# Moving the loads of x, half of the low parts, one norm and one sigmoid in a transformer block with 32 experts

## The chip, the cores and the metric

One Trainium2 chip, one core. The metric is the device time of one execution in microseconds (us). The kernel works in float32 throughout; its projections run as pairs of rounded operands (fp32r), as told below.

## What is computed

The reference is one encoder block over 256 tokens of width 1024: a joint projection, differential attention (4 heads) and neighbourhood attention (8 heads) on its columns, a gated merge, a residual with layer norm, and then a mixture of 32 experts with the best 4 for each token.

```python
proj = x @ w_in + b_in                          # 1024 -> 5120 columns
q_da, k_da, v_da, q_na, k_na, v_na, gate_pre = split(proj)
q_da, k_da = rope(q_da), rope(k_da)
a  = diff_attention(q_da, k_da, v_da, lam, lam_init, subln_g)   # softmax, RMS norm per head
nb = neighbourhood_attention(q_na, k_na, v_na, rpb)             # softmax with a position bias
g  = sigmoid(gate_pre)                          # two gates of width 1024
merged = g[0] * (a @ w_branch_da) + g[1] * (nb @ w_branch_na)
x = layer_norm(alpha * x + merged @ w_out)
x = layer_norm(alpha * x + moe(x))              # top 4 of 32, clamped SwiGLU
```

## The kernel before

The weights come in through a ring of SBUF tiles of 2 MB each, loaded by SP's queue in the order of their use. The first 28 pieces of 1 MB are called blocks here: blocks 0 to 19 are the ten column groups of `w_in` (two blocks a group: the first and the second half of the 1024 input rows), 20 to 23 the two branch matrices, 24 to 27 `w_out`. Behind them come the experts' weights, 403 MB. `refill` loads a ring tile again once TensorE is through with both of its blocks.

For accuracy each block is split into a rounded high part and the remainder, the low part: `split(i)` works in two halves of 128x1024, `act` on ScalarE (ACT) makes the high part, `tt` on VectorE (DVE) subtracts it from the block to make the low part. There are two tiles of split parts (`SPL = 2`), so block i's split can start when TensorE has done block i - 2. x goes the same way (`XH`, `XL`). A projection is then three products: high by high, low by high, high by low. Of a block's 48 matmuls (24 wider ones where the result is a value matrix, groups 2 and 5, that is blocks 4, 5, 10 and 11) the first half needs the first half of the split alone.

At the start, `feed` issues block 0 in four pieces of 256 KB, and after each the matching quarter of x (`load_x`); blocks 1 and 2 come in two pieces each. Block 0 uses the first half of x, block 1 the second.

Between the blocks the loop at the end of this stage calls what `at(key, ...)` has put down: after block 2 and block 4 the rotary embedding (`rope`: 14 DVE products and sums, seven for each pair of heads), after 6 to 9 the scores and the softmax of a differential head and after 7 to 10 its transpose, after 12 the RMS norm of the heads in two pairs (`da_norm`: a matmul of ones with the squares, a square root on ACT, a reciprocal, a scaling and a split on DVE), after 12, 13, 15 and 16 the neighbourhood heads (`na_bias` adds a mask to the bias on GpSimd, `na_softmax` goes to DVE and ACT), after 18 the sigmoid of gate "a", after 20 the router's loads. A planner of the framework orders the instructions of each engine's queue from their place in the program and from its own estimate of when they are ready; the order isn't written out by hand up to the end of `w_out`. On each engine instructions then run strictly in queue order. The order of the expert stage is written out by hand.

GpSimd (POOL in the profile) has little to do: the constants, two small loads into `gbx` at the start, and the eight bias adds of `na_bias`. `tp` and `pv` are PSUM tiles with one buffer each, `tp` used by the transposes, `pv` by the attention outputs.

The profile gives all of `act` as line L43 and all of `tt` as L46; the names of the tiles tell them apart: `sp` are the split parts, `qb`, `tm`, `qq` the rotary embedding, `pr`, `w`, `sm` the softmax, `tm<-tm` at L389 the reciprocal of the norm.

Of the kernel before, what the change touches and what calls it, by code (L numbers as in the profile page):

```python
# [9 lines left out]
F32 = mybir.dt.float32  # L10
# [3 lines left out]
ALU = mybir.AluOpType  # L14
# [17 lines left out]
def block_kernel(ctx: ExitStack, tc: tile.TileContext, x, xT, w_in, cols_in, b_v, lam_v,  # L32
# [9 lines left out]
    def act(o, i, f=AF.Copy, **kw):  # L42
        return nc.scalar.activation(o, i, f, **kw)  # L43

    def tt(o, a, b, op):
        return nc.vector.tensor_tensor(out=o, in0=a, in1=b, op=op)  # L46
# [41 lines left out]
    def feed(where=ring_tile):  # L88

        if not queue:  # L90
            return
        u = queue.pop(0)
        t = where()
        home[u] = where
        for s in range(2):
            ring[2 * u + s] = t[:, s * 2048:(s + 1) * 2048]
        if 2 * u < N1:
            for i in (2 * u, 2 * u + 1):
                src, k = chunks[i]
                v = ring[i].rearrange("p (k c) -> p k c", k=k)  # L100
                if i == 0:
                    for j in range(4):
                        nc.sync.dma_start(v[:, j], src[:, j])
                        load_x(j)
                elif i < 3:
                    for j in range(2):
                        nc.sync.dma_start(v[:, 2 * j:2 * j + 2], src[:, 2 * j:2 * j + 2])
                else:
                    nc.sync.dma_start(v, src)
            return  # L110
        kind, e, c = expert_unit(u)
        if kind == "m1":
            nc.sync.dma_start(t.rearrange("p (r c) -> p r c", r=2), m1c(e, c // 2))
        else:
            v, src = t.rearrange("p (k c) -> p k c", k=4), m2c(e, c // 2)
            n = 2 if e == NE - 1 else 4
            for k in range(0, 4, n):
                nc.sync.dma_start(v[:, k:k + n], src[:, k:k + n])
# [37 lines left out]
        t = splp.tile([128, 2, 2, 1024], F32R, name="sp", tag="sp")  # L156
        return [[t[:, u, n] for n in range(2)] for u in range(2)]

    def split(i):

        if i < N1 and (i, 0) not in parts:
            t = split_tile()
            for u in range(2):
                s = ring[i][:, u * 1024:(u + 1) * 1024]
                ws = t[u]
                act(ws[0], s)
                tt(ws[1], s, ws[0].bitcast(F32), ALU.subtract)
                k = chunks[i][1] // 2
                parts[i, u] = [w.rearrange("p (k c) -> p k c", k=k) for w in ws]

# [52 lines left out]
    def load_x(q):  # L223
        nc.sync.dma_start(xTt[:, 2 * q:2 * q + 2],
                          xT[256 * q:256 * q + 256, :].rearrange("(k p) t -> p k t", p=128))
# [15 lines left out]

    XH = big.tile([128, 8, T], F32R, name="XH", tag="xh")
    XL = big.tile([128, 8, T], F32R, name="XL", tag="xl")
    w0 = [[w.rearrange("p (k c) -> p k c", k=2) for w in ws] for ws in split_tile()]
    for j in range(4):
        u, r = divmod(j, 2)
        v = ring[0][:, j * 512:(j + 1) * 512]
        parts[0, u] = w0[u]
        act(w0[u][0][:, r], v)
        tt(w0[u][1][:, r], v, w0[u][0][:, r].bitcast(F32), ALU.subtract)  # L250
        s = slice(2 * j, 2 * j + 2)
        act(XH[:, s], xTt[:, s])
        tt(XL[:, s], xTt[:, s], XH[:, s].bitcast(F32), ALU.subtract)


    nlam = p1.tile([128, 1], F32, name="nlam")
# [125 lines left out]

    def da_norm(u):
        hh = slice(2 * u, 2 * u + 2)
        ms = pp.tile([128, 2, T], F32, name="tp", bufs=1)
        nc.tensor.matmul(ms, lhsT=ones, rhs=sq[:, hh], start=True, stop=True)
        rs = p1.tile([128, 2, T], F32, name="tm", tag="w", bufs=2)
        act(rs, ms, AF.Sqrt, scale=1.0 / 128.0, bias=eps)
        nc.vector.reciprocal(out=rs, in_=rs)  # L389
        nc.vector.scalar_tensor_tensor(out=rs, in0=aT[:, hh], scalar=gcol, in1=rs,  # L390
                                       op0=ALU.mult, op1=ALU.mult)
        act(AH[:, hh], rs)
        tt(AL[:, hh], rs, AH[:, hh].bitcast(F32), ALU.subtract)
# [20 lines left out]
    def na_softmax(h):  # L414
# [4 lines left out]
        sm = p1.tile([128, 4, 2], F32, name="sm", bufs=4)  # L419
        nc.vector.tensor_reduce(out=sm[:, 0], in_=s, axis=AX.X, op=ALU.max)  # L420
        nc.vector.tensor_scalar(sm[:, 1], sm[:, 0], -1.0, None, op0=ALU.mult)
        w = p1.tile([128, 2, T], F32, name="w", bufs=2)
        W["n", h] = w
        for q in range(2):
# [94 lines left out]
    def router_loads():  # L519
        nc.sync.dma_start(wr, w_router.rearrange("(k p) e -> p k e", p=128))  # L520
        nc.sync.dma_start(br[:, 0], b_router.rearrange("(o e) -> o e", o=1))

        for j, src in enumerate((ln1_g, ln1_b)):
            nc.gpsimd.dma_start(gbx[:, j].rearrange("p (c r) -> p c r", r=2), src.rearrange("(c p r) -> p c r", p=128, r=2))

    def router_fold():

# [15 lines left out]
    at(8, evac_t, 3, qk_na[:, 0:4])  # L543
    at(10, evac_t, 4, qk_na[:, 4:8])
    at(12, evac_v, 5, 1)
    at(12, da_norm, 0)
    at(12, da_norm, 1)
    at(12, na_alloc)
    for p, i in enumerate((12, 13, 15, 16)):
# [8 lines left out]
    at(14, gate, "a", 6, 0, AF.Identity)  # L558
    at(16, gate, "a", 7, 1, AF.Identity)
    at(17, gate_alloc, "b")  # L560
    at(18, lambda: act(G["a"], G["a"], AF.Sigmoid))
    at(18, gate, "b", 8, 0, AF.Sigmoid)
    at(20, gate, "b", 9, 1, AF.Sigmoid)
    at(21, gate_a, 0)
# [6 lines left out]
    at(23, lambda: preload(AF.Sqrt, G["b"][0:1, 7, 0:1]))  # L571

    for i in range(N1):
        if i + 1 < N1:
            split(i + 1)
        if i < 20:
            (proj_v if i // 2 in (2, 5) else proj_t)(i)
# [594 lines left out]
```

## Time and profile before

| | |
|---|---|
| time, median of 3 runs | 1151.42 us (1150.56 to 1152.11) |
| the profiled execution, its time | 1151.79 us |
| its span, first to last instruction | 1149.7 us |
| TensorE busy in the span | 93% |
| DVE, ACT, GpSimd busy | 32%, 22%, 2% |
| mean granted TensorE clock | 0.992 |
| read from memory | 437.86 MB, 382 GB/s over the span |

TensorE's busy share is that of pipelined matmuls whose ends are modelled, so 93% doesn't say that TensorE is at its peak. The projections, the attention and `w_out` end at about 202 us; the experts take the rest. In the rows below a line of the timeline gives the start, the duration, the engine, the line of the kernel, the operation, the output and its inputs, the shape and the count of instructions merged into it; in square brackets stands how long the engine had been idle before it and what ended that.

### The profile page before, as it was taken

How to read it: one execution, taken by the hardware profiler on the slowest of the kernel's cores; microseconds unless marked ns; L12 is line 12 of the kernel's file. 1: busy time of each engine (PE TensorE's matmuls, PEld its weight loads, DVE VectorE, ACT ScalarE, POOL GpSimd, SP SyncE). 2: the span in 40 equal slices, each digit the busy share in tenths (PEclk: the TensorE clock that was granted, in tenths of full speed). 3: DMA queues.
4: the chain of work that ended last, by engine and by line, in shares of the span. 5: the costliest groups of instructions: out<-in, count | busy, mean ns of one | idle time of the engine just before them, and what ended most of it. 6: DMA issues, size and time to landing. Idle time of an engine off the chain costs nothing.

```text
span 1149.7 us, 13448 instructions
## 1 busy us (share of the span) xinstructions
PE 1071.6 (93%) x5596; PEld 518.7 (45%) x5596; DVE 370.6 (32%) x786; ACT 258.3 (22%) x519; POOL 21.3 (2%) x30
## 2 busy tenths in 40 slices
PE   8999999999999999999999999998998899999884
PEld 8888898543334333333333333333333333333221
DVE  6977757223222222222222222222221222222213
ACT  5475853311111112122111111111111111111011
POOL 0001100000000000000000000000000000000001
PEclk9999999899999999999999999999999999999998
DMA  9953468799999999999999999999999999999991
GB/s 336 385 178 105 171 229 350 287 428 422 427 427 425 430 410 427 426 428 427 425 430 427 428 426 426 427 428 428 428 427 428 425 429 428 428 426 426 429 408 57
DMA packets 50787, 439.83 MB, mean 383 GB/s; under 512 B 5666, under 2 KB 8866, under 8 KB 23458
## 3 DMA queue, kind: packets, MB, share of 16 engines
q1 hardware_dynamic: 50098, 437.86, 91.9%
q8 instruction: 46, 0.75, 0.3%
q0 software_dynamic: 336, 0.54, 0.2%
q10 hardware_dynamic: 288, 0.52, 0.1%
q14 instruction: 19, 0.16, 0.0%
HBM read 437.86 MB, written 1.05 MB: 382 GB/s over the span
## 4 chain that ended last, share of the span: by engine, by line
DMA 45%; PE 44%; issue 4%; DVE 3%; ACT 2%; SPq 0%; POOL 0%; POOLq 0%; ACTq 0%
DMA ring<-in_w_dram 43%; PE sc L805 17%; PE tp L850 8%; PE pj L285 5%; PE pj L469 2%; PE tp L740 2%; PE sc L824 1%; PE pv L740 1%; DMA ring<-in_w_in_dram 1%; PE pj L873 1%; PE pj L300 1%; PE sc L510 1%; DVE tm L46 1%; ACT sp L43 1%; PE pv L884 1%
## 5 line engine op out<-in xcount | busy, mean ns | idle before, releaser
L805 PE MATMUL sc<-ring,XS 128*64 128x512 f32 x2048 | 473.7, 600 | 34.9 <-DMA ring<-in_w_dram 31.1
L805 PEld LDWEIGHTS sc<-ring,XS 128*64 128x64 f32 x2048 | 137.8, 137 | 305.0 <-issue 250.0
L850 PE MATMUL tp<-ring,hsas 128*64 128x512 f32 x1024 | 234.6, 598 | 12.2 <-DMA ring<-in_w_dram 11.7
L850 PEld LDWEIGHTS tp<-ring,hsas 128*64 128x64 f32 x1024 | 69.1, 136 | 150.7 <-issue 121.0
L813 DVE COPY hsas<-sc 128x512 f32<-128x512 f32 x32 | 22.1, 692 | 306.8 <-PE sc L805 306.8
L43 ACT ACTIVATE XS<-tp,gbx 128x128 f32<-128x128 f32 x64 | 25.8, 453 | 361.6 <-PE tp L740 359.8
L285 PE MATMUL pj<-XH,sp 128*128 128x256 f32 x512 | 96.3, 287 | 4.6 <-DVE sp L46 4.1
L285 PEld LDWEIGHTS pj<-XH,sp 128*128 128x128 f32 x512 | 80.1, 191 | 9.3 <-DVE sp L46 5.3
L46 DVE TENSOR_TENSOR sp<-ring,sp 128x1024 fp32r<-128x1024 f32 (+1 forms) x58 | 68.2, 1189 | 27.5 <-ACT sp L43 27.2
L771 DVE TENSOR_SCALAR GT<-pv,slotp 128x256 fp32r<-128x256 f32 x32 | 15.5, 484 | 186.7 <-PE pv L769 186.7
L43 ACT ACTIVATE sp<-ring 128x1024 fp32r<-128x1024 f32 (+1 forms) x58 | 58.0, 1023 | 67.5 <-PE pj L285 31.0
L285 PE MATMUL pj<-XL,sp 128*128 128x256 f32 x256 | 73.1, 286 | 0.1
L46 DVE TENSOR_TENSOR gl<-sc,bT 128x512 f32<-128x512 f32 x62 | 42.6, 688 | 64.8 <-PE sc L824 64.8
L43 ACT ACTIVATE as<-gl 128x256 f32<-128x256 f32 x64 | 26.7, 416 | 152.8 <-DVE gl L831 152.8
L863 DVE SCALAR_TENSOR_TENSOR ol<-tp,GS,oh 128x512 fp32r<-128x512 f32 x32 | 24.0, 751 | 99.3 <-ACT oh L43 99.3
L285 PEld LDWEIGHTS pj<-XL,sp 128*128 128x128 f32 x256 | 49.0, 191 | 0.9 <-issue 0.6
L43 ACT ACTIVATE oh<-tp,GS 128x512 fp32r<-128x512 f32 x32 | 22.0, 687 | 110.7 <-PE tp L850 110.7
L740 PEld LDWEIGHTS tp<-P,xres 128*128 128x128 f32 x256 | 33.4, 200 | 24.6 <-issue 24.3
L824 PEld LDWEIGHTS sc<-ident,hsas 128*128 128x128 f32 x248 | 32.3, 210 | 25.2 <-issue 25.2
L43 ACT ACTIVATE hsas<-sc 128x512 f32<-128x512 f32 x32 | 19.1, 597 | 103.6 <-PE sc L805 103.6
L740 PE MATMUL tp<-P,xres 128*128 128x128 f32 x256 | 39.4, 298 | 0.1
L824 PE MATMUL sc<-ident,hsas 128*128 128x128 f32 x248 | 38.2, 297 | 0.0
(213 smaller groups left out, 770.5 us busy)
## 6 DMA issues: line engine op xcount, KB each, us to landing
ring<-in_w_dram SPq DMA_DIRECT2D x171, 2048.0 KB, 34.2
ring<-in_w_dram SPq DMA_DIRECT2D x42, 1024.0 KB, 34.2
ring<-in_w_in_dram SPq DMA_DIRECT2D x17, 1024.0 KB, 13.8
ring<-in_w_out_dram SPq DMA_DIRECT2D x4, 1024.0 KB, 6.3
ring<-in_w_in_dram SPq DMA_DIRECT2D x4, 512.0 KB, 8.0
nb<-in_rpbx_dram SPq DMA_DIRECT2D x8, 256.0 KB, 3.4
ring<-in_w_da_dram SPq DMA_DIRECT2D x2, 1024.0 KB, 5.2
ring<-in_w_na_dram SPq DMA_DIRECT2D x2, 1024.0 KB, 7.8
```

Source lines behind the costliest of these rows:

```text
L43: return nc.scalar.activation(o, i, f, **kw)
L46: return nc.vector.tensor_tensor(out=o, in0=a, in1=b, op=op)
L285: nc.tensor.matmul(pj[g][:, c], lhsT=a(k, cc), rhs=b[:, kk], start=(kk == 0 and j == 0 and c % 2 == 0), stop=(kk == 7 and j == 2), skip_gr ...
L300: nc.tensor.matmul(pj[g][:, h], lhsT=a[:, kk, hh], rhs=b(k), start=(kk == 0 and j == 0), stop=(kk == 7 and j == 2), skip_group_check=True)
L469: nc.tensor.matmul(y[:, c], lhsT=a(k, cc), rhs=b[:, k], start=(k == 0 and j == 0 and c % 2 == 0), stop=(k == 3 and j == 2), skip_group_che ...
L740: nc.tensor.matmul(px[:, u], lhsT=v, rhs=P[g][:, t], start=(t == 0), stop=(t == 1))
L771: nc.vector.tensor_scalar(GT[e], p[:, 256:512], slotp[:, 0:1], None, op0=ALU.is_equal)
L805: nc.tensor.matmul(HP[h][j * CAP:(j + 1) * CAP], lhsT=XS[e // 2][:, c, e % 2], rhs=w[:, h, j], start=(c == 0), stop=(c == 7), skip_group_c ...
L813: nc.vector.tensor_copy(HS[e][:, 1], HP[1])
L824: nc.tensor.transpose(p[:, s, k], v[:, s, k], ident)
L850: nc.tensor.matmul(OP[e][j * CAP:(j + 1) * CAP], lhsT=AS[e][:, c, k], rhs=ring[i][:, n:n + 512], start=(c + k == 0), stop=(c == 3 and k == ...
L863: nc.vector.scalar_tensor_tensor(out=ol, in0=OP[e], scalar=GS[e], in1=oh.bitcast(F32), op0=ALU.mult, op1=ALU.subtract)
```

## The change

Five edits, all ahead of the expert stage.

- The quarters of x are loaded behind pieces 0 and 2 of block 0 and behind the two halves of block 1, and split there too (`split_x`, called through the new argument `also` of `split`), where before each stood behind one piece of block 0.
- In blocks 2 to 10 the second half's low part is subtracted on GpSimd and not on DVE.
- `da_norm(0)` is called after block 10 instead of 12, and `da_norm(1)` uses the PSUM tile `pv`.
- The sigmoid of gate "a" gets a zero bias that is made from the last neighbourhood head's negated maximum (h = 7), and so can't run before that is there.
- The two loads into `gbx` go from GpSimd's queue to SP's.

```diff
@@ feed
                 if i == 0:
                     for j in range(4):
                         nc.sync.dma_start(v[:, j], src[:, j])
-                        load_x(j)
+                        if j in (0, 2):
+                            load_x(j // 2)
                 elif i < 3:
                     for j in range(2):
                         nc.sync.dma_start(v[:, 2 * j:2 * j + 2], src[:, 2 * j:2 * j + 2])
+                        if i == 1:
+                            load_x(2 + j)
@@ split
-    def split(i):
+    def split(i, also=lambda q: None):
...
                 act(ws[0], s)
-                tt(ws[1], s, ws[0].bitcast(F32), ALU.subtract)
+                e = nc.gpsimd if u == 1 and 1 < i < 11 else nc.vector
+                e.tensor_tensor(out=ws[1], in0=s, in1=ws[0].bitcast(F32), op=ALU.subtract)
+                also(2 + u)
@@ the split of x
+    def split_x(q):
+        s = slice(2 * q, 2 * q + 2)
+        act(XH[:, s], xTt[:, s])
+        tt(XL[:, s], xTt[:, s], XH[:, s].bitcast(F32), ALU.subtract)
...
-        s = slice(2 * j, 2 * j + 2)
-        act(XH[:, s], xTt[:, s])
-        tt(XL[:, s], xTt[:, s], XH[:, s].bitcast(F32), ALU.subtract)
+        if j in (0, 2):
+            split_x(j // 2)
@@ da_norm
-        ms = pp.tile([128, 2, T], F32, name="tp", bufs=1)
+        ms = pp.tile([128, 2, T], F32, name=("tp", "pv")[u], bufs=1)
@@ na_softmax
         nc.vector.tensor_scalar(sm[:, 1], sm[:, 0], -1.0, None, op0=ALU.mult)
+        if h == 7:
+            late["zero"] = keep.tile([128, 1], F32, name="zero")
+            nc.vector.tensor_scalar(late["zero"], sm[:, 1, 1:2], 0.0, None, op0=ALU.mult)
@@ router_loads
-            nc.gpsimd.dma_start(gbx[:, j].rearrange("p (c r) -> p c r", r=2), src.rearrange("(c p r) -> p c r", p=128, r=2))
+            nc.sync.dma_start(gbx[:, j].rearrange("p (c r) -> p c r", r=2), src.rearrange("(c p r) -> p c r", p=128, r=2))
@@ the calls between the blocks
-    at(12, da_norm, 0)
+    at(10, da_norm, 0)
     at(12, da_norm, 1)
...
-    at(18, lambda: act(G["a"], G["a"], AF.Sigmoid))
+    at(18, lambda: act(G["a"], G["a"], AF.Sigmoid, bias=late["zero"]))
...
     for i in range(N1):
-        if i + 1 < N1:
+        if i == 0:
+            split(1, split_x)
+        elif i + 1 < N1:
             split(i + 1)
```

## Rows read from the trace of the kernel before

**Rows 1.** Stretch, its length; busy PE, PEld, DVE, ACT, POOL; clock; DMA share, GB/s.

```profile
70.00:80.00 10.00, 9.83 (x64) 8.16 (x63) 7.29 (x15) 7.41 (x22) 2.65 (x2) 1.00 0.39 93
...
400.00:1100.00 700.00, 651.52 (x3127) 251.41 (x3123) 159.19 (x384) 99.30 (x222) 2.18 (x5) 1.00 1.01 427
```

**Rows 2.** TensorE's timeline: matmuls at which a wait ended.

```profile
14.68 0.38 PE L285 MATMUL pj<-XH,sp 128*128 128x256 f32 x1 [0.88 <-DVE sp L46]
...
32.98 0.50 PE L300 MATMUL pj<-sp,XH 128*128 128x512 f32 x1 [0.66 <-DVE sp L46]
...
45.88 0.39 PE L285 MATMUL pj<-XH,sp 128*128 128x256 f32 x1 [1.17 <-DVE sp L46]
...
99.20 1.13 PE L386 MATMUL tp<-aTsq,ones 128*128 128x512 f32 x2 [0.43 <-ACT tm L43]
...
111.22 0.39 PE L285 MATMUL pj<-XH,sp 128*128 128x256 f32 x1 [1.49 <-DVE sp L46]
...
134.40 0.70 PE L367 MATMUL tp<-ident,w 128*128 128x128 f32 x4 [1.02 <-DVE w L428]
```

**Rows 3.** ACT's timeline at the start: the high parts of block 1.

```profile
12.31 1.06 ACT L43 ACTIVATE sp<-ring 128x1024 fp32r<-128x1024 f32 x1 [0.73 <-DMA ring<-in_w_in_dram]
...
13.67 1.06 ACT L43 ACTIVATE sp<-ring 128x1024 fp32r<-128x1024 f32 x1 [0.30 <-DMA ring<-in_w_in_dram]
```

**Rows 4.** SP's timeline: router bias, and the next issue.

```profile
65.91 2.72 SPq L521 DMA_DIRECT2D br<-in_b_router_dram  x1
...
77.71 0.38 SPq L109 DMA_DIRECT2D ring<-in_w_da_dram  x1
```

**Rows 5.** Timelines of GpSimd and DVE where they overlap.

```profile
116.05 1.83 POOL L402 TENSOR_TENSOR nb<-nb,cst 128x512 f32<-128x512 f32 x1 [10.94 <-DMA nb<-in_rpbx_dram]
...
117.44 1.53 DVE L46 TENSOR_TENSOR sp<-ring,sp 128x1024 fp32r<-128x1024 f32 x1
...
118.86 1.29 POOL L402 TENSOR_TENSOR nb<-nb,cst 128x512 f32<-128x512 f32 x1 [0.98 <-DMA nb<-in_rpbx_dram]
...
118.89 1.41 DVE L428 TENSOR_SCALAR w<-w,sm 128x256 f32<-128x256 f32 x1
```

**Rows 6.** DVE's timeline around the rotary embedding.

```profile
24.09 2.77 DVE L46 TENSOR_TENSOR tm<-qb,cst 32x512 f32<-32x512 f32 x4
...
31.70 1.22 DVE L46 TENSOR_TENSOR sp<-ring,sp 128x1024 fp32r<-128x1024 f32 x1
...
44.61 1.22 DVE L46 TENSOR_TENSOR sp<-ring,sp 128x1024 fp32r<-128x1024 f32 x1
```

**Rows 7.** ACT's timeline: the splits of blocks 3 and 5.

```profile
20.61 2.01 ACT L43 ACTIVATE sp<-ring 128x1024 fp32r<-128x1024 f32 x2 [3.18 <-PE pj L285]
...
32.13 2.01 ACT L43 ACTIVATE sp<-ring 128x1024 fp32r<-128x1024 f32 x2 [3.75 <-PE pj L285]
```

**Rows 8.** DVE's and TensorE's timelines at head 0's softmax.

```profile
55.02 0.15 DVE L349 TENSOR_SCALAR sm<-sm 128x2 f32<-128x2 f32 x1
...
57.17 0.88 DVE L359 SCALAR_TENSOR_TENSOR w<-pr,sm 128x256 f32<-128x256 f32 x2
...
58.18 0.60 PE L367 MATMUL tp<-ident,w 128*128 128x128 f32 x4
```

**Rows 9.** Busy time by stretch at the end of the span.

```profile
1135.00:1138.40 3.40, 0.47 (x4) 0.03 (x2) 1.30 (x2) 0.54 (x1) 0.00 (x0) 1.00 0.02 7
...
1138.40:1145.00 6.60, 0.00 (x0) 0.00 (x0) 5.71 (x13) 1.26 (x3) 1.63 (x2) 0.50 0.17 62
```

**Rows 10.** DVE's timeline at the norm.

```profile
99.52 6.55 DVE L389 RECIPROCAL tm<-tm 128x512 f32<-128x512 f32 x2
...
109.95 1.22 DVE L46 TENSOR_TENSOR sp<-ring,sp 128x1024 fp32r<-128x1024 f32 x1
```

**Rows 11.** ACT's timeline at the sigmoid.

```profile
129.45 1.92 ACT L43 ACTIVATE qq<-qq 128x2048 f32<-128x2048 f32 x1
...
131.37 1.28 ACT L43 ACT_TABLE_LOAD   x1
```

## The prediction

> **What bounds the kernel now.** I read the table by stages first. In the expert stage the DMA engines are busy all the time at 427 GB/s, while in the projection stage at 70 to 80 us they are busy 0.39 of the time [rows 1]. The DMA queue there waits for ring tiles that TensorE must release, so a microsecond that TensorE gains or loses in the projections moves the whole weight stream, and the end, by a microsecond; a share gained on another engine is worth nothing by itself. The question is therefore which waits of TensorE the change removes or adds before about 200 us. Its timeline there shows waits that the edits touch: 0.88 us before the first half of block 1, 0.66 before block 4, 1.17 before block 6, 0.43 at the second norm matmul, 1.49 inside block 14, 1.02 at a neighbourhood transpose [rows 2]. Together 5.65 us, 0.5% of the time.
>
> **Start.** In the old order all of x, between the pieces of block 0, is ahead of block 1, and block 1's first half is there at 12.31 us; its split takes ACT 1.06 us, and the first low part lets TensorE go on at 14.68 [rows 2, 3]. The next 512 KB, its second half, land 1.36 us behind it [rows 3]. In the new order that first half has 512 KB less ahead of it (x2 and x3 come behind each half), so it lands about 1.36 us earlier, at 10.95. ACT then ends its high part at 12.0, DVE its low part at 13.25, and then comes the new last step, the low part of x2 (0.69 us for 512 columns), at 13.95. TensorE's third matmul waits for that. Instead of 14.68 it goes on at about 13.85: **-0.85 us**. Ends: 0 if x2 lands late enough to eat it, -1.36 if all of the landing counts. The two gbx loads leave GpSimd's queue for SP. There the nearest row is the router bias, which takes SP 2.72 us from 65.91; SP's next issue is at 77.71 [rows 4]. Two such issues, 5.4 us, fit into that pause, and the stage has idle DMA time [rows 1]: nothing. Without that pause they would hold two ring loads for up to 5.4 us.
>
> **Low parts on GpSimd.** First what one costs. GpSimd's nearest row is the bias add, 1.29 us for 128x512 (at 118.86, ahead of the DVE instruction that wanted to run) [rows 5]. For 128x1024 that bounds it by 1.29 and 2.58; it has twice the columns, so I take 2.4, against 1.22 on DVE. Then whether the two engines run side by side. They don't: a bias add that starts during a DVE subtraction takes 1.83 instead of 1.29, a DVE subtraction that starts under that add takes 1.53 instead of 1.22, and a 256-column scaling that starts under the next add takes 1.41 [rows 5], where two heavier 256-column products take 0.88 [rows 8]. Each waits until the other is through. At 118.86 GpSimd asks while DVE is in a subtraction, and goes ahead of the DVE instruction queued behind it: DVE's stream doesn't keep it out.
>
> The Trainium skill says the same in SBUF — State Buffer, "Who interferes with whom": a DVE instruction with two SBUF inputs and a GpSimd one that reads SBUF exclude each other for the whole instruction, and whichever issues first goes. The rows agree (1.83 for 1.29). By that rule this edit moves 1.2 us of DVE work to where it blocks DVE for 2.4. The Trainium skill's GPSIMD Engine Reference, "Performance versus the Vector engine", gives 4497 ns for an add over 2048 columns; half of it, 2.25 us, is an estimate for our size, and no row has it. With it each of the four low parts below is 0.15 cheaper, 0.6 us in the sum.
>
> Now the walk, in the old clock. From 24.09 to 44.61 us DVE does nothing but subtractions of splits and the rotary products, all with two SBUF operands and back to back; the planner put eleven products of 0.69 (24.09 to 31.70, 7.6 us) ahead of block 4's first low part, and eleven again ahead of block 6's at 44.61 [rows 6]. TensorE needs exactly that first low part to start a block, and the second only 2.9 us later (half a block; two blocks lie between 20.61 and 32.13 [rows 7]). GpSimd's half is the one that isn't urgent, yet it asks first.
> - Block 1 ends at 19.75 (20.61 less 0.85). ACT splits block 3 in 2.0 us [rows 7]; DVE ends its first low part at 22.0, GpSimd's second holds DVE out to 24.4.
> - The products need 7.6 us. Block 4's split is ready at 27.5, block 5's at 33.25 (ACT starts them as blocks 2 and 3 end; block 3 ends at 32.13 [rows 7], less the shift 31.25). Both GpSimd parts get in between: 24.4 + 7.6 + 2.4 + 2.4 = 36.8. Then block 4's first low part, 1.2: 38.0. Block 4 starts 5.0 us later than at 32.98, and TensorE idles for 6.7.
> - Blocks 4 and 5 with head 0's first scores take 11.7 us (from 32.98 to the wait that ends at 45.88 [rows 2]): 49.7. The second set of products starts at 39.9 (38.0, the last product's 0.7, block 5's first part), needs 7.6 plus 2.4 for block 6's GpSimd half: 49.9. Block 6's low part ends at 51.1, where TensorE now goes on at 45.88: **+5.2 us**, the start's gain already in it.
> - Blocks 7 to 10 meet the softmaxes. For head 0 the small scaling at 55.02 stands on DVE behind block 8's low part, and the head's last product starts at 57.17 and just makes the transpose at 58.18 [rows 8]. GpSimd's half of block 8 is ready at 53.85 (block 6 ends 5.9 us after 45.88, the split takes 2.0), waits for DVE until 54.85 and runs to 57.25; the scaling, and with it two exponentials, two reciprocals and four products, waits: 57.2 for 55.1, **+1.9** after the 0.15 us that the chain has spare. For heads 1 and 2 the bounds are 0 and 1.9 each, by head 0; there GpSimd's half falls where DVE's own second subtraction stood, so I take +0.1 for both.
> - Clock. The granted clock fell to half at 1138.4 after 3.4 us in which TensorE was busy for 0.47, and stayed there for the 6.6 us of that row [rows 9]. Before block 4 TensorE would idle for twice as long. Half speed over 6.6 us costs 3.3, of which block 6's late low part covers 1.4 (49.7 to 51.1): between 0 and +1.9, and since one fall at the tail is all that speaks for it, **+1.0**.
>
> **Norm.** Two reciprocals stand in DVE's queue from 99.52 for 6.55 us, and behind them block 14's second low part at 109.95, for which TensorE waits 1.49 us [rows 2, 10]. With the first heads' norm issued behind block 10, one of them (3.3 us) moves two blocks up, beside the 5.8 us of block 11's matmuls; what it delays there are low parts that are due a block later (without that cover it would cost its 3.3). Block 14's low part is 3.3 us earlier, so all 1.49 go. The second norm matmul has a PSUM tile of its own and drops its 0.43. **-1.92.** What pays is ACT: one table load (1.28 us) comes earlier, none is added if the square root lies behind head 3's exponentials. Next late would be the exponentials behind it, which also come 3.3 us earlier.
>
> **Sigmoid.** It runs at 129.45 for 1.92 us, and behind it ACT loads the exponentials' table again, 1.28 [rows 11]; the transpose of what they make waits 1.02 [rows 2]. Bound to the last head's maximum it comes behind the last exponentials, where its load serves the other gate too; a split behind it starts a block (5.76 us) ahead of its use and needs 2.0 on ACT and 1.2 on DVE, so 1.92 fit. **-1.02**; at worst 0. The added one-column product is under 0.2 us of DVE, off the chain.
>
> **Sum:** 5.2 + 1.9 + 0.1 + 1.0 - 1.92 - 1.02 = +5.3 us. The profiled execution took 1151.79 (span 1149.70 and 2.09 around it), 0.37 over the median, so 1151.42 + 5.3 = 1156.7.
>
> **Rivals.**
> - *GpSimd's half is hidden.* No row shows the 32-partition products or this size under a GpSimd instruction; if they pass each other, TensorE's 0.66 and 1.17 go as well as the rest: -0.85 - 0.66 - 1.17 - 1.92 - 1.02 = -5.6, 1145.8. For it: DVE is indeed the late one at both blocks. Against it: all overlaps in rows 5. It decides against me once the products keep their 0.69 us under GpSimd. This one is faster.
> - *Only one GpSimd half gets in ahead of each urgent low part*, because DVE's queue or the planner's order lets the low part pass: 2.4 us less, no fall of the clock. Block 6 then starts 2.8 us late, and 2.8 + 2.0 - 2.94 = +1.9, 1153.3.
> - *The change doesn't do what it says at the norm:* the planner puts the early square root before head 3's exponentials, 2 x 1.28 more for the table on ACT in front of a chain without slack: 1156.7 + 2.6 = 1159.3.
>
> **How the numbers follow.** Forecast 0.49 (its own range 1153.7 to 1160.5: without the clock's 1.0 and with the start's full landing, 0.5 more, it is 1155.2; with no start gain and the clock's full price 1158.4; without the sigmoid's gain as well 1159.5; about 1 us on both sides for the order), hidden 0.30, one half 0.13, square root 0.08. A difference under 0.2% (2.3 us) can't be told from none, so same is 1149.1 to 1153.7. Slower 0.49 + 0.08 = 0.57, same 0.12, faster 0.30 + 0.01 = 0.31. The range reaches to the hidden case: 1145.0 to 1160.5.
>
> **What would show it.** Right: products of 0.69 us stretched to about 3 us where a GpSimd subtraction lies, TensorE's wait before block 4 at 5 us or more, GpSimd's parts at 2.4 us. Wrong: both blocks starting without a wait while GpSimd works, or block 4's low part ahead of the products. The norm's step is right if the 1.49 is gone and one reciprocal lies before block 12, the sigmoid's if ACT loads tables twice less, the start's if block 1 goes on near 13.9.

## The result and the profile after

The changed kernel takes 1161.56 us (median of four runs, 1160.19 to 1162.40), the kernel before beside it 1151.15. The medians lie 10.4 us apart; the ratio of the runs, which is used from here on, is 1.0082 with a 95% interval of 1.0067 to 1.0097, or 9.4 us slower. Below, a ratio is always against the kernel before on the same chip, and 0.001 is 1.15 us. The profiled execution took 1160.87 us with a span of 1159.2, 9.5 more than before's 1149.7.

DVE's and GpSimd's timelines of the changed kernel beside the rotary embedding, which answer to [rows 6]:

```profile
21.75 2.49 POOL L172 TENSOR_TENSOR sp<-ring,sp 128x1024 fp32r<-128x1024 f32 x1 [2.77 <-ACT sp L43]
22.43 4.45 DVE L46 TENSOR_TENSOR tm<-qb,cst 32x512 f32<-32x512 f32 x4 [0.45 <-ACT qb L43]
26.70 2.43 POOL L172 TENSOR_TENSOR sp<-ring,sp 128x1024 fp32r<-128x1024 f32 x1 [2.46 <-ACT sp L43]
26.88 2.80 DVE L46 TENSOR_TENSOR qq<-qb,cst 128x512 f32<-128x512 f32 x1
...
31.11 4.24 DVE L46 TENSOR_TENSOR tm<-qb,cst 32x512 f32<-32x512 f32 x3
32.46 2.34 POOL L172 TENSOR_TENSOR sp<-ring,sp 128x1024 fp32r<-128x1024 f32 x1 [3.33 <-ACT sp L43]
35.36 0.69 DVE L46 TENSOR_TENSOR qq<-qb,cst 128x512 f32<-128x512 f32 x1
35.97 1.22 DVE L172 TENSOR_TENSOR sp<-ring,sp 128x1024 fp32r<-128x1024 f32 x1
...
46.73 2.77 POOL L172 TENSOR_TENSOR sp<-ring,sp 128x1024 fp32r<-128x1024 f32 x1 [11.94 <-ACT sp L43]
47.15 3.42 DVE L172 TENSOR_TENSOR sp<-ring,sp 128x1024 fp32r<-128x1024 f32 x1
```

One set of rotary products and sums is twelve instructions, six for each pair of heads (not fourteen and seven, as said above). Three GpSimd halves, of blocks 3, 4 and 5, lie in the first set, and a DVE instruction that falls under one isn't through until about 0.55 us behind it (29.68 for 29.13, 35.35 for 34.80): four products take 4.45 for 2.77, one takes 2.80 for 0.69, three take 4.24 for 2.08. Block 4's low part runs at 35.97, and block 6's at 47.15 is itself held by block 6's own GpSimd half. TensorE's timeline, the places where a wait ended, for [rows 2, 8]:

```profile
12.93 0.39 PE L296 MATMUL pj<-XL,sp 128*128 128x256 f32 x1 [0.22 <-DVE XL L46]
...
37.24 0.80 PE L311 MATMUL pj<-sp,XH 128*128 128x512 f32 x1 [6.78 <-DVE sp L172]
...
50.63 0.39 PE L296 MATMUL pj<-XH,sp 128*128 128x256 f32 x1 [0.57 <-DVE sp L172]
...
64.73 0.41 PE L378 MATMUL tp<-ident,w 128*128 128x128 f32 x2 [1.21 <-DVE w L370]
...
118.56 0.33 PE L378 MATMUL tp<-ident,w 128*128 128x128 f32 x1 [2.36 <-DVE w L442]
...
1117.64 1.94 PE L867 MATMUL tp<-ring,hsas 128*64 128x512 f32 x8 [1.20 <-DMA ring<-in_w_dram]
```

The 0.88 at the start is 0.22, the 1.17 before block 6 is 0.57, and 1.49, 0.43 and 1.02 are gone; before block 4 stands 6.78 for 0.66, and 1.21 and 2.36 are new. The last row is TensorE's last wait for weights: in the kernel before it ended at 1109.92. Busy time by stretch (length; PE, PEld, DVE, ACT, POOL; clock; DMA share, GB/s), for [rows 1, 9]:

```profile
34.13:40.96 6.83, 3.72 (x9) 2.98 (x10) 6.72 (x11) 1.04 (x3) 0.67 (x1) 0.50 1.05 388
119.47:122.88 3.41, 3.41 (x18) 3.41 (x18) 2.52 (x7) 2.71 (x9) 1.71 (x1) 0.50 0.50 150
400.00:1100.00 700.00, 653.65 (x3124) 252.01 (x3122) 159.03 (x382) 99.95 (x223) 2.06 (x4) 1.00 1.01 426
1126.39:1129.80 3.41, 3.41 (x9) 0.86 (x6) 0.00 (x0) 0.40 (x1) 0.00 (x0) 0.50 0.59 240
```

The clock falls to half (1.2 GHz) at 34.13, in the wait before block 4, at 119.47, 0.9 us behind the wait of 2.36, and in the tail at 1126.39; before's has none of these three. The weight stream runs at 426 GB/s where the row of before says 427; a difference of this size comes up again below.

How far TensorE lies behind the kernel before, read from the starts of the same matmuls in both traces: 4.75 us at block 6 (45.88 to 50.63), 6.55 at head 0's transpose (58.18 to 64.73), 6.7 at the end of block 10 (82.50 to 89.19), 7.4 at block 19 (150.05 to 157.48), 6.2 at the first experts (252.28 to 258.48, a matmul of the second; before's clock had been at half for 6.8 us at 210, the changed kernel's for 3.4 at 218), 8.0 at the last experts (1060.54 to 1068.56, a matmul of the last but one), 9.5 at the end. These two matmuls are meant below by the first and the last experts.

### The profile page after: what moved, and what is told of

Its sections match the earlier page's. It is cut to its first block, busy times and chain, and to the rows that moved or that the text cites. A ratio compares the mean times of both kernels' runs of the same rounds, so it can differ in the third digit from the quotient of the medians.

```text
span 1159.2 us, 13465 instructions
## 1 busy us (share of the span) xinstructions
PE 1077.8 (93%) x5596; PEld 522.9 (45%) x5596; DVE 376.3 (32%) x778; ACT 255.9 (22%) x517; POOL 42.0 (4%) x37
## 4 chain that ended last, share of the span: by engine, by line
PE 45%; DMA 45%; issue 4%; DVE 4%; ACT 1%; POOL 0%; SPq 0%; POOLq 0%; ACTq 0%
DMA ring<-in_w_dram 42%; PE sc L822 17%; PE tp L867 8%; PE pj L296 5%; PE pj L483 2%; PE tp L757 2%; PE sc L841 1%; PE pv L757 1%; DVE tm L46 1%; PE pj L890 1%; DMA ring<-in_w_in_dram 1%; PE sc L524 1%; DVE sp L172 1%; PE pv L901 1%; PE pj L311 1%
## 5 line engine op out<-in xcount | busy, mean ns | idle before, releaser
L172 DVE TENSOR_TENSOR sp<-ring,sp 128x1024 fp32r<-128x1024 f32 x45 | 59.7, 1337 | 21.9 <-ACT sp L43 21.8
```

Of the source, the lines that this page charges most:

```text
L172: e.tensor_tensor(out=ws[1], in0=s, in1=ws[0].bitcast(F32), op=ALU.subtract)
```

## The experiments

### What GpSimd's halves cost

The changed kernel with its low parts back on DVE:

```diff
-                e = nc.gpsimd if u == 1 and 1 < i < 11 else nc.vector
+                e = nc.vector
```

> The changed kernel with its low parts of blocks 2 to 10 back on DVE. Theory (GpSimd's halves shut DVE out and take their turn ahead of the urgent first low part): the whole loss comes from them, so TensorE starts block 4 and block 6 as in the kernel before less the start's 1.85 us (waits of about 0.7 and 1.2 us), head 0 has no wait, and the time is 1151.2 - 1.9 (start) - 1.0 (sigmoid) and 0 to -1.9 for the norm: 1146.4 to 1148.3. Rival (the other four edits share in the loss, by the planner's new order of TensorE's queue at block 14): about 1151 to 1153, with the wait of about 2.4 us before the second half of block 14 still there.

Measured: ratio 1.0019 (1.0010 to 1.0029). Blocks 4 and 6 wait 1.73 and 0.74, and head 0 no longer waits, but 2.42 us stand before the second half of block 14. TensorE is 1.1 us ahead at the first experts (251.14) and 1.0 behind at the last. So GpSimd makes 0.0063 of the 0.0082, 7.3 us, and the other four edits don't gain the 3.8 us of the forecast: they lose 2.2. The rival was right that they share in the loss and that the wait at block 14 stands, but its reason isn't the whole: TensorE comes to the experts early all the same, and what is lost is lost behind that (see the address, below).

The other way round, the kernel before with GpSimd's halves only, in blocks 2 to 10 (the diff), in 3 to 6 (`2 < i < 7`) and in 7 to 10 (`6 < i < 11`):

```diff
-                tt(ws[1], s, ws[0].bitcast(F32), ALU.subtract)
+                e = nc.gpsimd if u == 1 and 1 < i < 11 else nc.vector
+                e.tensor_tensor(out=ws[1], in0=s, in1=ws[0].bitcast(F32), op=ALU.subtract)
```

> The kernel before with GpSimd's halves of blocks 2 to 10 alone. Theory (exclusion and order): in the changed kernel block 6 started 4.75 us late with 1.85 gained at the start, so 6.6 us, plus 1.2 at head 0: TensorE is 7.8 us late at the end of block 10, and the time 1158 to 1161, TensorE's wait before block 4 near 8 us. Rival (GpSimd's half is merely 1.2 us slower than DVE's, the engines pass each other): no wait before a first half grows, and the time stays within 2 us of 1151.

> As the run with all of GpSimd's halves, but in blocks 3 to 6 alone, beside the rotary embedding. Theory: nearly the whole loss lies here, +6.6 us at block 6, 1157 to 1159. Rival (the loss is spread over all halves alike, each 1.2 us slower): 4 of 9 of it, about +3, 1154.

> As the run with all of GpSimd's halves, but in blocks 7 to 10 alone, beside the heads' softmaxes. Theory: only head 0's chain has no room, +1.2 us there, heads 1 and 2 nothing: 1151.5 to 1153. Rival (alike for all halves): 4 of 9 of the loss, about +3, 1154 to 1155.

Measured: 1.0068 (1.0051 to 1.0084), 1.0070 (1.0052 to 1.0089) and 1.0019 (1.0010 to 1.0029). The wait before block 4 is 5.86 with all halves, not near 8. By the times blocks 3 to 6 alone make all of it, with a wait of 5.92 before block 4; by the traces they make 6.2 of the 7.4 us at the first experts. Blocks 7 to 10 cost 2.2 us, more than the 1.2 expected: beside 1.48 at head 0's transpose, TensorE waits 0.82 inside block 6, because block 7's GpSimd half (from 45.52) stretches a low part of block 6 (3.42 for 1.22, from 45.81). The parts don't add up to the whole (2.2 and 8.1 to 7.8; at the first experts 2.3 and 6.2 to 7.4). In the times that is within the intervals; in the traces head 0 waits 1.48 with the later halves alone and 1.21 with all, so the later waits are partly covered where the first set has delayed TensorE.

### Exclusion, or only a late result?

No instruction uses what GpSimd writes here (into a tile `scratch` of the last pool); all low parts are on DVE:

```diff
                 tt(ws[1], s, ws[0].bitcast(F32), ALU.subtract)
+                if u == 1 and 2 < i < 7:
+                    for n in range(2):
+                        c = slice(512 * n, 512 * n + 512)
+                        nc.gpsimd.tensor_tensor(out=scratch, in0=s[:, c], in1=ws[0].bitcast(F32)[:, c], op=ALU.subtract)
```

> The kernel before, every low part still on DVE; beside the second half of blocks 3 to 6 GpSimd does work that nobody uses: two subtractions of 128x512 that read the same block and high part. Theory (a GpSimd instruction that reads two SBUF operands shuts DVE out for its time, and gets its turn between DVE's queued products): each pair takes 2.6 us from DVE on top of its own 1.2, so TensorE's waits before blocks 4 and 6 grow by about 7 and a few us, 1158 to 1161. Rival (the loss comes from what waits for GpSimd's result): nothing waits for it here, so 1151 to 1152.

and with fills in place of the subtractions:

```diff
+                    nc.gpsimd.tensor_scalar(scratch[:, 0:1], ws[0].bitcast(F32)[:, 0:1], 1.0, None, op0=ALU.mult)
+                    for n in range(4):
+                        nc.gpsimd.memset(scratch, 0.0)
```

> As the run with GpSimd's unused subtractions, but with one one-column product and four fills of 128x512 with zero instead, which write as many bytes and more and read nothing from SBUF. Theory (what shuts DVE out is the reading of SBUF): DVE's products keep their 0.69 us, 1151 to 1152. Rival (any busy GpSimd slows DVE): products stretched and TensorE waiting before block 4 as in the other run.

Measured: 1.0072 (1.0057 to 1.0088) with the subtractions, 0.9990 (0.9981 to 0.9999) with the fills. Timeline with the subtractions:

```profile
22.42 3.61 POOL L171 TENSOR_TENSOR scratch<-ring,sp 128x512 f32<-128x512 f32 x2 [18.72 <-ACT sp L43]
24.91 3.75 DVE L46 TENSOR_TENSOR tm<-qb,cst 32x512 f32<-32x512 f32 x4
...
38.70 0.79 PE L305 MATMUL pj<-sp,XH 128*128 128x512 f32 x1 [6.66 <-DVE sp L46]
```

and with the fills:

```profile
22.11 2.28 POOL L171 MEMSET scratch<- 128x512 f32 x4
23.14 2.77 DVE L46 TENSOR_TENSOR tm<-qb,cst 32x512 f32<-32x512 f32 x4
25.92 0.69 DVE L46 TENSOR_TENSOR qq<-qb,cst 128x512 f32<-128x512 f32 x1
```

With the subtractions the whole wait before block 4 is back, with no result awaited; four fills beside the same products leave them at 0.69 each. The exclusion is shown, and that it comes with GpSimd's reading. (Two of ACT's splits wait until GpSimd has read the tile that they overwrite, at 31.89 and 51.62; neither is the split of block 4 or 6.) It also agrees with the Trainium skill, SBUF — State Buffer, "Who interferes with whom", by which a GpSimd instruction that only writes SBUF doesn't contend with a DVE instruction that has two SBUF inputs.

### Does it need the order of DVE's queue?

GpSimd's halves of blocks 2 to 10, and each set of rotary products called a block later:

```diff
-    at(2, rope, qk_da[:, 0:4], 0)
+    at(3, rope, qk_da[:, 0:4], 0)
...
-    at(4, rope, qk_da[:, 4:8], 1)
+    at(5, rope, qk_da[:, 4:8], 1)
```

> GpSimd's halves of blocks 2 to 10 as in the run with them alone, and the two sets of rotary products called one block later each, so that the planner puts the low parts of blocks 4 and 6 ahead of most of them. Theory (the loss needs both the exclusion and a queue in which products that aren't urgent stand ahead of the urgent low part): the waits before blocks 4 and 6 fall to 1 to 3 us together from 8, 1152 to 1155. Rival (the exclusion alone is enough): 1158 and more.

Measured: 1.0060 (1.0046 to 1.0075), not distinct from 1.0068. TensorE's timeline:

```profile
32.97 0.50 PE L301 MATMUL pj<-sp,XH 128*128 128x512 f32 x1 [0.91 <-DVE sp L168]
40.22 0.50 PE L301 MATMUL pj<-sp,XH 128*128 128x512 f32 x1 [1.52 <-DVE sp L168]
48.63 0.39 PE L286 MATMUL pj<-XH,sp 128*128 128x256 f32 x1 [2.76 <-DVE sp L168]
...
64.24 0.74 PE L368 MATMUL tp<-ident,w 128*128 128x128 f32 x4 [1.21 <-DVE w L360]
```

The low part of block 4 now comes ahead of most products, as meant, and the wait before it is 0.91 instead of 5.86. The time returns in four smaller places: 0.25, 1.52, 1.59 and 1.21 us over before, 4.6 in all, and the clock at half for 3.4 us at about 50. My theory fell here: the loss needs no unlucky queue. In neither of the two orders has DVE time to give between block 3 and block 6. The kernel with the later products and without GpSimd's halves, its proper partner, wasn't run by itself; a version below that has them with the new start waits before neither block.

### The start

The kernel before with the order and split of x (the diff of the change) and gbx on SP:

> The kernel before with the new order and split of x and the two gbx loads on SP, nothing else. Both theories: block 1 goes on near 12.9 us, the projections end 1.8 us earlier. Theory A (a gain before the experts moves the weight stream and the end): 1149.5, ratio 0.998. Theory B (the stream of expert weights, not TensorE, paces the second half of the experts, and what is gained ahead isn't kept there): 1151 to 1152, the lead of 1.8 us still there at the first 15 experts and gone at the last ones.

Measured: 0.9992 (0.9983 to 1.0001). Block 1 goes on at 12.83. Over all kernels here, those with the new order go on at 12.6 to 13.6 (seven, mean 13.1), those with the old at 13.5 to 14.7 (thirteen, mean 14.2): a gain of 1.1. Some is lost again at once: block 4 waits 1.55 instead of 0.66, since ACT's split of block 3 now waits for its load (until 19.55) and DVE's products come only 1.06 us earlier (23.03 for 24.09). Neither theory is settled by this time.

### The norm

The kernel before with the two edits of `da_norm`:

> The kernel before with the two edits at the norm alone (called behind block 10, second PSUM tile). Prediction's step: 1.49 and 0.43 us of waits go, TensorE is 1.92 us earlier at block 14. Rival (the planner puts the first neighbourhood transposes ahead of block 14's second half on TensorE, and their softmax stands behind the second reciprocal on DVE): a new wait of about 2.4 us there, TensorE 0.5 us later and, with a fall of its clock, up to 2 us later: 1151.5 to 1153.

and with these lines added, which bring the transposes of neighbourhood heads 0 and 1, and all that belongs to heads 2 and 3, one block later:

```diff
-    for p, i in enumerate((12, 13, 15, 16)):
+    for p, i in enumerate((12, 14, 15, 16)):
...
-            at(i + 1, w_transpose, ("n", h))
+            at(i + (1 if p else 2), w_transpose, ("n", h))
```

> The two edits at the norm, and the softmaxes of neighbourhood heads 2 and 3 and the first four transposes called one block later. Theory (the step of the norm is right, and its gain was eaten by the place of the transposes on TensorE): no wait of 2.4 us, TensorE 1.5 to 1.9 us ahead of the kernel before at the end of block 14, unless the later softmaxes are late in turn. Rival (the norm itself has no gain): TensorE level with the kernel before there. The end of the program hardly shows it: 1150 to 1152.

Measured: 1.0003 for both (0.9994 and 0.9992 to 1.0013); the times don't separate them, the traces do. TensorE's timeline with the norm's edits alone, and after it with the later transposes:

```profile
110.68 0.69 PE L367 MATMUL tp<-ident,w 128*128 128x128 f32 x2 [2.40 <-DVE w L428]
```

```profile
107.78 0.39 PE L285 MATMUL pj<-XH,sp 128*128 128x256 f32 x1 [0.64 <-DVE sp L46]
112.65 0.55 PE L367 MATMUL tp<-ident,w 128*128 128x128 f32 x3 [0.78 <-ACT wt L43]
```

All that these edits move on TensorE lies between block 10 and block 19. The starts of the two, in the kernel before, with the edits alone, and with the later transposes:

```profile
76.89 0.74 PE L300 MATMUL pj<-sp,XH 128*128 128x512 f32 x2
150.05 0.50 PE L285 MATMUL pj<-XH,sp 128*128 128x256 f32 x2
```

```profile
75.73 0.73 PE L300 MATMUL pj<-sp,XH 128*128 128x512 f32 x2
150.31 0.50 PE L285 MATMUL pj<-XH,sp 128*128 128x256 f32 x2
```

```profile
75.98 0.73 PE L300 MATMUL pj<-sp,XH 128*128 128x512 f32 x2
148.43 0.50 PE L285 MATMUL pj<-XH,sp 128*128 128x256 f32 x2
```

TensorE needs 73.16, 74.58 and 72.45 us (73.0 to 73.3 in ten other kernels with the old norm, 74.3 and 74.6 in two whose clock falls on the way). So the edits alone lose 1.4 us, with the clock at half for 3.4 us at 110. The new place of the transposes on TensorE is what costs: called later, they leave a gain of 0.7. The 1.92 of the forecast isn't seen in any run. With the later transposes the 0.43 and the 1.02 are gone, but 0.64 of the 1.49 inside block 14 is left, and 0.78 stands before a transpose.

### The sigmoid, and the address of the ring

The kernel before with the sigmoid's bias alone, as in the change; then with the zero in the pool that is opened last; then an unused tile of one column, with no other edit; then the same with 16 columns (`[128, 16]`); then the changed kernel with its zero in the last pool:

```diff
-            late["zero"] = keep.tile([128, 1], F32, name="zero")
+            late["zero"] = p1.tile([128, 1], F32, name="zero")
```

```diff
     eps = keep.tile([128, 1], F32, name="eps")
+    pad = keep.tile([128, 1], F32, name="pad")
```

> The kernel before with the sigmoid's bias alone. Prediction's step: the 1.02 us before the neighbourhood transpose goes, two table loads fewer, 1150 to 1150.5 if the gain reaches the end, 1151 if it doesn't. Beside that it tells whether the new one-column tile, which moves the addresses of what is allocated behind it, costs the weight stream anything: it moved 426.1 GB/s from 350 to 1100 us in the two kernels that have this tile, 426.5 to 426.7 in the four that don't. If the tile does it, 426.1 here as well, 0.9 us more over the experts, and 1151 to 1152.

> The sigmoid's bias alone, with the zero in the pool that is opened last, so that no other address moves. Theory of the address: 426.5 to 426.7 GB/s, the 1.02 us before the neighbourhood transpose gone, and 0 to 1 us faster than before, 1.0 to 2.5 us faster than the same edit with the tile in the first pool (1153.6 there beside 1151.8 of before). Rival (chance): the two alike.

> The kernel before with one unused one-column tile beside eps, which moves the SBUF addresses of the ring, the split parts and all behind them from 21824 to 21856 bytes (a multiple of 64 before, of 32 alone now); no instruction differs. Theory (the address is what costs the three kernels with the tile their weight stream): 426.1 GB/s from 350 to 1100 us, 0.9 to 1.5 us longer, ratio 1.001. Rival (the rate differs from run to run by chance): 426.5 to 426.7 as in the kernels without the tile, the time within 0.5 us.

> The kernel before with an unused tile of 16 columns beside eps, so that the ring begins at 21888 bytes: as in the run with one unused column every address behind it is moved, but it stays a multiple of 64. Theory (a ring that begins at a multiple of 32 and not of 64 is what costs 2.4 to 3.6 us): 427 GB/s in the row from 350 to 1100 us, the time as before, 1151 to 1152.5. Rival (any move of the addresses costs, or the choice of before is a lucky one): 1153.5 to 1156.

> The changed kernel with its zero tile in the pool that is opened last, so that the ring keeps its old addresses. Theory (the one-column tile cost 2 to 4 us through the ring's addresses): 427 GB/s in the row from 350 to 1100 us instead of 426, TensorE's lag of 6.2 us at the first experts stays at 6 to 7 to the end, 1158 to 1159.5, ratio to the kernel before 1.006. Rival (the surplus comes from the lag itself or by chance): 1161 to 1162 as the changed kernel.

| kernel | ring begins at | GB/s, 350 to 1100 us | ratio |
|---|---|---|---|
| before with the sigmoid, zero in the first pool | 21856 | 426.1 | 1.0013 (1.0004 to 1.0022) |
| before with the sigmoid, zero in the last pool | 21824 | 426.6 | 0.9992 (0.9980 to 1.0004) |
| before with an unused column | 21856 | 426.1 | 1.0031 (1.0019 to 1.0042) |
| before with 16 unused columns | 21888 | 426.2 | 1.0019 (1.0003 to 1.0035) |
| the change | 21856 | 426.2 | 1.0082 (1.0067 to 1.0097) |
| the change, zero in the last pool | 21824 | 426.6 | 1.0060 (1.0047 to 1.0073) |

The rates are means over 150 slices of 5 us. Of all twenty kernels the five with a moved ring have 426.1 to 426.2, the other fifteen 426.5 to 426.7. Busy time by stretch, first of the sigmoid with its zero in the last pool, then of the kernel with one unused column:

```profile
350.00:1100.00 750.00, 702.52 (x3372) 271.73 (x3368) 170.83 (x412) 106.67 (x238) 2.08 (x4) 1.00 1.01 427
```

```profile
350.00:1100.00 750.00, 700.84 (x3370) 270.95 (x3366) 170.82 (x412) 106.76 (x238) 2.08 (x4) 1.00 1.01 426
```

An unused tile of four bytes in each partition costs 3.6 us (0.9 to 1.5 were expected), one of 64 bytes 2.2, and where the same edit is made with and without the shift the difference is 2.4 (sigmoid) and 2.5 us (the whole change, where the two intervals still overlap). Hence in the changed kernel about 2.5 us come from where `zero` was put, not from what it does. The rate explains 0.8 of it (0.1% of 750 us): from the first to the last experts the five kernels with a moved ring lose 1.8 to 2.1 us against the trace of before, the other fourteen 0.0 to 1.4. The rest is seen in the tail, where the clock is at half once more than before, as in the changed kernel at 1126.39. All five with a moved ring have such a fall, of 3.4 to 13.7 us, and need 26.0 to 30.3 us from the last matmul of the experts' first layer to the last of their second; of the other fifteen, ten have none and need 24.4, five have one of 3.4 or 6.8 us and need 26.0 to 27.8. One stretch of the tail, first in the kernel before, then in the one with an unused column:

```profile
1120.16:1126.99 6.83, 6.31 (x25) 1.84 (x25) 0.75 (x1) 1.88 (x3) 0.00 (x0) 1.00 0.27 110
```

```profile
1120.16:1126.99 6.83, 6.83 (x14) 1.27 (x10) 0.00 (x0) 0.60 (x1) 0.00 (x0) 0.50 0.29 118
```

With one trace of each kernel, how often such a fall comes with and without the shift stays open.

The cause within the address is open, and also which tile makes it: the split parts and all else behind the ring move with it. My theory was the multiple of 64; the ring at 21888 is one and is slow as well, so that fell. The Trainium skill's DMA: Bandwidth & Descriptors, "How a descriptor splits into AXI transactions", says that a transaction has to start on a 256-byte boundary and that bytes fetched ahead of a start off it still cost beats. It speaks of what is fetched, where the ring is what is written, and no run here shows it: the three addresses lie 64, 96 and 128 bytes behind a boundary, and a ring on one wasn't tried.

The sigmoid itself, without the shift, gives nothing that can be measured. The trace shows why: the 1.02 is gone, but from the end of block 16 to the next attention output TensorE needs 9.00 us as before (132.32 to 141.32, and 132.25 to 141.25), since the order now has transposes ahead of the scores and breaks the scores in two:

```profile
132.32 0.60 PE L367 MATMUL tp<-ident,w 128*128 128x128 f32 x4
132.85 1.13 PE L411 MATMUL sc<-qq 64*128 64x256 f32 x6
134.16 0.66 PE L367 MATMUL tp<-ident,w 128*128 128x128 f32 x4 [0.19 <-ACT wt L43]
134.75 0.70 PE L411 MATMUL sc<-qq 64*128 64x256 f32 x2
```

(the zero in the first pool). Before, such a set of transposes stood between matmuls of block 17 and took 0.4 of its time (134.40 to 134.85 for the first).

### Versions that keep what helps

The kernel before with the order of x, gbx on SP, the sigmoid with its zero in the last pool, and both sets of rotary products a block later; then the same with the norm's edits and later transposes but only the first set moved; then that with both sets moved. All pieces are in the diffs above.

> The kernel before with the order of x, gbx on SP, the sigmoid's bias with its zero in the pool opened last, and the rotary products one block later; no GpSimd halves, no edit at the norm. If the waits before blocks 4 and 6 go and the start's gain of 1.85 us passes them, TensorE is 1.85 + 0.66 + 1.17 + 1.02 = 4.7 us ahead at block 16. Theory A (the weight stream moves with it): 1147 to 1149. Theory B (the expert stream starts from a full ring and keeps its pace): 1150 to 1151.

> The earlier version (order of x, gbx on SP, sigmoid with its zero in the last pool) with the norm's edits and later transposes, and only the first set of rotary products one block later. If each place keeps what it showed alone (1.3 us at the start less what block 4 and 6 take back, 1.9 at the norm, 1.0 at the sigmoid) and the gain moves the weight stream: 1147.5 to 1149.5. Rival (gains ahead of the experts are taken back): 1150.5 to 1152.

> As the one before it, with both sets of rotary products one block later. The wait of 2.1 us at head 0 should stand here as in the earlier version, since the second set then falls beside head 0's softmax, while block 6 waits for nothing: level with the other, 1147.5 to 1149.5; rival as there.

Measured: 0.9983 (0.9973 to 0.9993), 0.9987 (0.9978 to 0.9996) and 0.9977 (0.9964 to 0.9990). The last is 2.6 us faster than the kernel before, the three not distinct from one another, and the first two not from the 0.9990 that the kernel with unused fills came to. TensorE is 0.9, 3.4 and 2.1 us ahead at the first experts; with both sets moved head 0 waits 2.1 us, as expected. Of the 3.39, 2.06 is left at the last experts. There twelve of the fourteen kernels with an unmoved ring stand 0.8 to 1.4 us later against the trace of before than at the first experts, those that lag as those that lead (the two with GpSimd's unused work 0.5 and 0.0), so this is no loss of the gain.

For delays theory A holds: kernels that are 2.3, 6.2, 7.4 and 9.7 us late at the first experts (halves of blocks 7 to 10, 3 to 6, all, unused subtractions) take 2.2, 8.1, 7.8 and 8.3 us longer. For gains of 1 to 3 us the times don't settle it: 3.4 us of lead go with 1.5 us of time, 2.1 with 2.6, and the 1.8 of the norm with later transposes with none.

## Why the prediction was wrong in its size

The sign and the main mechanism were right, the time (1156.7 for 1161.56, just above the range) wasn't. Two steps failed: the gain at the norm and the sigmoid, and the tile `zero`, which the sum had at nothing. By its steps:

| step | forecast | in the two traces |
|---|---|---|
| start | -0.85 | -1.75; -1.1 over all kernels |
| GpSimd at blocks 4 and 6, with the start | +5.2 | +4.75 |
| head 0 | +1.9 | +1.8 |
| heads 1 and 2 | +0.1 | +0.1 |
| clock | +1.0 | nothing beyond the +4.75 |
| norm and sigmoid | -2.94 | +0.75 |
| behind block 19 | 0 | +2.1 |

- **GpSimd, right.** 2.34 to 2.49 us for 2.4, products stretched to 2.80, a wait of 6.78 for 6.7, block 4 at 37.24 for 38.0, all as walked. That the wait came so close is partly luck: block 1 went on 0.9 us earlier than walked and block 4 0.8. One reason was idle: "it asks first" and the planner's order are how it went, not why, as the later products showed.
- **Clock, mis-sized.** It fell at 34.13, as feared, and was back at 40.96; block 6 then still waited 0.57 for its low part, which stood behind DVE's products and GpSimd's half, so the price was covered and not only 1.4 of it. That is read from the trace; no run kept the clock up. It needn't be so: with `zero` moved the fall came at 35.34, and block 6 then waited for nothing. The one fall that the forecast went by was not the only one in the kernel before, whose clock was at half for 6.8 us at 210 too.
- **Norm, the first step that failed.** The waits of 1.49 and 0.43 went, as said. The sentence "next late would be the exponentials ..., which also come 3.3 us earlier" looked at ACT and DVE and not at TensorE's own queue: there the transposes of these heads now stand right behind block 14's first half (that the planner's estimates saw the heads ready sooner is the likely reason, not a shown one). DVE's and GpSimd's timelines in the changed kernel show what they then waited for:

```profile
106.21 3.34 DVE L400 RECIPROCAL tm<-tm 128x512 f32<-128x512 f32 x1
...
112.91 1.29 POOL L413 TENSOR_TENSOR nb<-nb,cst 128x512 f32<-128x512 f32 x1 [4.12 <-DMA nb<-in_rpbx_dram]
113.13 2.15 DVE L172 TENSOR_TENSOR sp<-ring,sp 128x1024 fp32r<-128x1024 f32 x1
114.81 1.62 POOL L413 TENSOR_TENSOR nb<-nb,cst 128x512 f32<-128x512 f32 x1 [0.61 <-DMA nb<-in_rpbx_dram]
115.20 1.25 DVE L432 TENSOR_SCALAR sm<-sm 128x2 f32<-128x2 f32 x1
116.37 1.21 DVE L172 TENSOR_TENSOR sp<-ring,sp 128x1024 fp32r<-128x1024 f32 x1
...
118.16 0.60 DVE L442 TENSOR_SCALAR w<-w,sm 128x256 f32<-128x256 f32 x2
```

The second reciprocal still lies there, and the bias adds hold a low part (2.15 for 1.22) and a two-column product (1.25). The wait of 2.36 and the clock at half behind it take the 1.92 back. Alone, the edits at the norm lose 1.4 us from block 10 to block 19; with the sigmoid's they come to +0.75 in the changed kernel (73.91 for 73.16), and to +0.1 where the clock doesn't fall there (73.30, with `zero` moved).
- **Sigmoid, mis-sized to zero.** It moved as said, with one table load at 147.22 ahead of it; the 1.02 went, and the planner's other order of the same matmuls took as long.
- **The tile `zero`, the second step that failed.** It was costed as "under 0.2 us of DVE". Its place in the pool ahead of the ring cost about 2.5 us. The two traces are level at the first experts (6.2 us behind, with `zero` in either pool); at the last they are 8.0 and 7.1 behind, at the end 9.5 and 6.4. The changed kernel without this comes to 1157.94 us (ratio 1.0060), 1.2 from the forecast and inside the range. That this is close is luck: the errors at the norm and the sigmoid (+3.7), and at the clock, the start and the first experts offset each other.
- **gbx on SP, right:** two issues of 0.50 and 0.62 us at 86.03 and 86.57, behind the router bias; the bound of 2.7 each was wide.
- **Rivals.** The hidden half is excluded by the stretched products; one half only, by three of them in the first set; at the norm a rival was named for ACT's tables, which didn't come (9 table loads for 11 before), while the one that came true sat on TensorE.

## What to carry to other kernels

Before half of a two-operand DVE step is given to GpSimd, look whether DVE has idle time there: if both read SBUF they take turns, and the move adds the difference of their speeds (2.4 for 1.2 us) to DVE's queue. When something is moved earlier under a planner, read the new order of the engine that sets the end before the gain is counted. A new tile ahead of a large streamed buffer moves all addresses behind it and is an edit of its own: put it behind, or test it alone.

## What the runs showed of the hardware that was not expected

- With the ring and all behind it shifted by 32 or 64 bytes the weight stream ran at 426.1 to 426.2 GB/s instead of 426.5 to 426.7 (five kernels against fifteen), and an unused tile that does no more made the kernel 3.6 and 2.2 us longer.
- GpSimd fills of 128x512 take 0.57 us each (2.28 for four) and don't disturb DVE's two-operand products at all.
- GpSimd's turn came at the next end of an instruction: in the changed kernel its halves beside the rotary products took 2.34 to 2.77 us, waiting included, where DVE had a queue of instructions ready, and 2.40 where DVE was idle (16.58).
- The start alone has about 1 us of play from trace to trace: block 1 goes on between 13.5 and 14.7 us in thirteen kernels that have the same instructions up to there.
